# Retention and neighbourhood stages of a two-block fp32 model: a pair's last norm deferred, bias tables and residual rows requested earlier

## The chip, the core and the metric

The program runs on one core of one Trainium2 chip. The metric is the device time of one execution in microseconds (us); the kernel before takes 3239.62 us, the median of 3 runs (3238.14 to 3244.05). Everything is fp32 in and out. A projection is split into rounded high and low parts, and three matmuls (high by high, high by low, low by high) make one.

## The reference, cut

Two blocks on a sequence of 1024 tokens and 1024 channels. The first (dilated attention, then a state-space layer) is not touched. The second has two hybrid layers, each with a convolution branch, a retention branch (6 heads of 64) and a neighbourhood attention branch (6 heads), on 1024 tokens and 256 context tokens; in the second layer the context has only keys and values.

```python
def head_norm(o):
    mu = jnp.mean(o, axis=-1, keepdims=True)
    var = jnp.mean(jnp.square(o - mu), axis=-1, keepdims=True)
    return (o - mu) * lax.rsqrt(var + LN_EPS)

# retention: queries and keys rotated, both directions, chunks of 128
o = bidir_retention(qh, kh, vh, lg_f, lg_b, s_f, s_b)
y_ret = from_heads(head_norm(o)) * jax.nn.silu(g)

# neighbourhood: window of 8 x 16 on the 16 x 64 grid, plus all context tokens
s_loc = einsum(q, k_win) * scale + rpb[:, dr + 7, d_col + 15]
s_ctx = einsum(q, k_ctx) * scale
p = softmax(concatenate([s_loc, s_ctx]))
y_na = (einsum(p_loc, v_win) + einsum(p_ctx, v_ctx)) * silu(g)

y = concatenate([y_conv, y_ret, y_na]) @ w_out
x_new = layer_norm(DEEPNORM_ALPHA * x + gate * y, ln_g, ln_b)
```

## The kernel before

The program is written for a framework that lays the instructions of each engine out with a timeline of its own, so the order in the code is a wish: what an engine gets can stand some places earlier or later. TensorE (PE) does the matmuls and the transposes, VectorE (DVE) and ScalarE (ACT) read PSUM and write SBUF, GpSimd (POOL) helps, and all DMAs go out on the in-order queue of SyncE (SP).

Nearly all of TensorE's work is projections: `mm3` (the matmuls are line 168) issues 24 matmuls of 128x512 (or 128x256 for the context) into one PSUM tile `mm`, which has two buffers. After every eighth matmul it calls `tick()`, which runs a closure of the list `hot` and, at the speed that `pace()` set, closures of the list `bg`: so the small steps of attention are strewn between the projections. `drain()` runs what is left in `bg` at once.

`hybrid(l)` is called for l = 0 (with context) and l = 1 (without context queries). After half of the convolution it runs `ret_pair(p)` for three pairs of heads. `ret_pair` first projects the gates (and ticks the background of the pair before), then drains, then projects values, keys and queries. `raw` evicts a projection into `raw` (four buffers) and hangs the follow-up into `hot`. Each of a pair's query groups (two of 512 tokens, and for l = 0 one of 256 context tokens) has five steps f1 to f5, which become the background of the *next* pair's gates: f1 and f2 rotate and transpose (lines 1463, 1494), f3 makes the scores (line 1588) and f4 the outputs (1603, 1606). The end of f4 is a chain over four engines: copy `oe` (ACT, 1609), transposes `O` (PE, 1612), squares (ACT, 1617), row sums (DVE, 1619), two small POOL steps (1620, 1621), `cen` (DVE, 1623). f5 is the next step: PE transposes `cen` (1632), DVE multiplies by the gate (1635) and SP stores `yd` (1636). At the end of a gate projection `drain()` puts the last f4 and the last f5 right behind each other.

After pair 2, `na_project(0)` projects gates, values, keys (`nk`) and queries (`nqq`, line 1428) of the neighbourhood branch, and `na_core(p)` runs pairs 0 to 2: `vturn` and `cturn` transpose the values (PE 1677 and 1684; DVE copies `nV` 1678 and `nVc` 1686). `tables(rt)` brings a bias table for row type rt: one `mask` (one buffer) and six pieces of `tab` (tab0 and tab1, two buffers each, line 1700), and then DVE adds the mask (1701). Eight units of 128 queries follow: scores `S` (PE 1734), DVE 1710 and 1714 (which reads `tab`), ACT 1717 (exponential), transposes `T` (PE 1747, 1748), copies `nPT` (DVE 1751, ACT 1753), products `O` (PE 132, 135).

`out_ln` (from line 1916) ends the layer: for each tile of 128 tokens it fetches `x` (line 1949), projects two halves of 512 channels, multiplies each by `gate` out of PSUM (DVE 1955), adds the residual and keeps a row sum (1956), and normalises (1967 to 1972).

```python
self.bg.extend(late[g][k] for g, k in turns if g < len(late))
...
out = [tables(0), vturn(0), vturn(1), cturn, vturn(2), vturn(3)]
...
if i == 2:
    tables(1)()
```

## Time and profile before

| | before |
|---|---|
| median of 3 runs | 3239.62 us (3238.14 to 3244.05) |
| the profiled execution, its own time | 3247.39 us |
| its span, first to last instruction | 3245.4 us |
| TensorE busy | 3119.8 us, 96% of the span |
| VectorE, ScalarE, GpSimd busy | 59%, 37%, 18% |
| mean granted TensorE clock | 0.986 |
| second block, layer 0 and layer 1 | from about 1770 to 2560 us, and on to the end |

The span is read from its densest engine. TensorE is hardly ever idle, so what counts is the list of waits in front of its instructions, and for each of them what the other engines did at that moment. "[4.13 <-DVE cen L1623]" behind an instruction says that its engine sat idle for 4.13 us before it and that DVE's instruction of line 1623, which writes `cen`, ended that. An SP row's duration is the time in which the queue issued the transfer, not the time until it landed.

### The profile page before, as it was taken

To read this page: it belongs to the slowest core of one execution; us is meant where nothing else is said; L and a number is where in the kernel's file an instruction comes from. 1 tells how busy PE (TensorE), PEld (TensorE's weight loads), DVE (VectorE), ACT (ScalarE), POOL (GpSimd) and SP (SyncE) were. 2 spreads that over 40 slices of the span, in tenths; PEclk is the share of its full clock that TensorE was granted. 3 is DMA by queue.
4 is the path that set the end of the run, shared out by engine and by line. 5 is a ranking of instruction groups with operands and counts; after the bars stand their busy time and mean duration, and the time that the engine had idled before them with its cause. 6 is when DMAs were issued, how large, how long until landed. Compare 5 with 4: busy or idle time off the path is not lost. (4 is left out here: it accounts for less than half of the span.)

```text
span 3245.4 us, 48179 instructions
## 1 busy us (share of the span) xinstructions
PE 3119.8 (96%) x18340; PEld 2576.7 (79%) x18340; DVE 1925.1 (59%) x4147; ACT 1210.5 (37%) x2496; POOL 578.3 (18%) x769
## 2 busy tenths in 40 slices
PE   7999999999999999999999999999999999999998
PEld 6888787877778788787878888778887888778777
DVE  5565668777775748565644634454557854445555
ACT  4544444444444554322432122244352212134351
POOL 1244402121111201111003023200002212210001
PEclk9999999999999999999999999999999999999999
DMA  4222233332322225565342211142224321133232
GB/s 137 59 86 91 83 92 100 97 95 87 99 88 72 74 90 179 182 176 156 130 136 91 66 46 50 48 119 73 73 80 161 101 69 56 46 101 88 72 113 97
DMA packets 325210, 312.86 MB, mean 96 GB/s; under 512 B 27801, under 2 KB 277364, under 8 KB 324980
## 3 DMA queue, kind: packets, MB, share of 16 engines
q1 hardware_dynamic: 324980, 309.80, 31.4%
q8 instruction: 144, 2.36, 0.3%
q14 instruction: 86, 0.70, 0.1%
HBM read 249.64 MB, written 60.09 MB: 95 GB/s over the span
## 5 line engine op out<-in xcount | busy, mean ns | idle before, releaser
L168 PE MATMUL mm<-aTh,wh 128*128 128x512 f32 (+1 forms) x2704 | 1076.6, 398 | 26.6 <-DVE qk L353 9.8
L168 PE MATMUL mm<-aTl,wh 128*128 128x512 f32 (+1 forms) x2704 | 1075.0, 398 | 0.7 <-DVE aTl L221 0.3
L168 PE MATMUL mm<-aTh,wl 128*128 128x512 f32 (+1 forms) x2704 | 1070.1, 396 | 0.8 <-DVE wl L155 0.8
L168 PEld LDWEIGHTS mm<-aTh,wh 128*128 128x128 f32 x2704 | 513.4, 190 | 136.4 <-issue 8.2
L168 PEld LDWEIGHTS mm<-aTh,wl 128*128 128x128 f32 x2704 | 513.2, 190 | 102.6 <-issue 3.7
L168 PEld LDWEIGHTS mm<-aTl,wh 128*128 128x128 f32 x2704 | 513.8, 190 | 100.6 <-issue 5.4
L155 DVE TENSOR_TENSOR wl<-wr,wh 128x1024 fp32r<-128x1024 f32 x176 | 220.9, 1256 | 183.8 <-ACT wh L154 181.9
L154 ACT ACTIVATE wh<-wr 128x1024 fp32r<-128x1024 f32 x176 | 186.0, 1057 | 362.9 <-PE mm L168 297.7
L414 ACT ACTIVATE sb<-sb,st 128x128 f32<-128x128 f32 (+1 forms) x384 | 170.4, 445 | 278.3 <-DVE st L412 277.0
L168 PE MATMUL mm<-wo,aTh 128*128 128x512 f32 x768 | 242.4, 397 | 7.9 <-DVE ys L1955 4.6
L412 DVE CUSTOM_DVE_ANT_0 sb<-S,bt 128x128 f32<-128x128 f32 (+1 forms) x384 | 126.4, 343 | 116.9 <-PE T L425 92.3
L1153 DVE SCALAR_TENSOR_TENSOR ma<-mw,cact,ma 128x256 f32<-128x256 f32 x336 | 174.0, 530 | 15.6 <-DMA mw<-in_w_mod 10.0
L168 PEld LDWEIGHTS mm<-wo,aTh 128*128 128x128 f32 x768 | 144.5, 190 | 38.7 <-DVE ys L1955 5.0
L168 PE MATMUL mm<-wo,aTl 128*128 128x512 f32 x384 | 151.8, 395 | 0.9 <-DVE aTl L1900 0.9
L1717 ACT ACTIVATE nsb<-nsb,nmn 128x640 f32<-128x640 f32 (+1 forms) x108 | 85.6, 793 | 117.9 <-DVE nmn L1714 105.5
L1160 POOL TENSOR_TENSOR ms<-ma,ms 128x256 fp32r<-128x256 f32 x48 | 40.2, 837 | 413.9 <-ACT ms L1159 301.8
L357 POOL CAST qk<-kz 64x512 fp32r<-64x512 f32 x64 | 65.8, 1028 | 252.7 <-ACT kz L351 250.6
L425 PE MATMUL T<-ident,sb 128*128 128x128 f32 x560 | 99.3, 279 | 11.9 <-ACT PT L428 8.1
L168 PE MATMUL mm<-cTh,wl 128*128 128x256 f32 x352 | 101.9, 289 | 0.6 <-DVE wl L155 0.6
L168 PE MATMUL mm<-cTl,wh 128*128 128x256 f32 x352 | 102.0, 290 | 0.0
L168 PE MATMUL mm<-cTh,wh 128*128 128x256 f32 x352 | 101.4, 288 | 0.0
L1710 DVE CUSTOM_DVE_ANT_0 nsb<-S,zero 128x256 f32<-128x256 f32 x108 | 45.0, 421 | 84.2 <-PE T L1748 30.3
(443 smaller groups left out, 5221.1 us busy)
## 6 DMA issues: line engine op xcount, KB each, us to landing
wr<-in_attn_w_in SPq DMA_DIRECT2D x80, 512.0 KB
wr<-in_w_in SPq DMA_DIRECT2D x64, 512.0 KB
mw<-in_w_mod SPq DMA_DIRECT2D x48, 512.0 KB
tab<-in_c_rpb SPq DMA_DIRECT2D x72, 192.0 KB
Wb<-wgd SPq DMA_DIRECT2D x96, 128.0 KB
x<-x SPq DMA_DIRECT2D x24, 512.0 KB
x<-in_x SPq DMA_DIRECT2D x16, 512.0 KB
wr<-in_ssm_w_in SPq DMA_DIRECT2D x16, 512.0 KB
```

Of the source, the lines that this page charges most:

```text
L154: nc.scalar.activation(h, raw, AF.Copy)
L155: nc.vector.tensor_tensor(l, raw, h.bitcast(F32), op=ALU.subtract)
L168: nc.tensor.matmul(out, s_, m_, start=first and i == 0, stop=last and i == len(todo) - 1)
L357: nc.gpsimd.tensor_copy(at(t[o], g, hf), at(h_[r], g, hf))
L412: nc.vector.tensor_tensor_reduce(out=sb[:, :N], in0=sp[:, a * 256:a * 256 + N], in1=b, scale=1.0, scalar=3e38, op0=ALU.add, op1=ALU.min, a ...
L414: nc.scalar.activation(sb[:, :N], sb[:, :N], AF.Exp, bias=mc, scale=-1.0, accum_out=st[:, 1, g, a, n:n + 1])
L425: nc.tensor.transpose(t[:, c:c + 128], Ps[a][:, b * 128:b * 128 + 128], self.ident)
L1153: V.scalar_tensor_tensor(a, L[h][:, k], c, a, op0=ALU.mult, op1=ALU.add)
L1160: nc.gpsimd.tensor_tensor(l_, L["a", i], h.bitcast(F32), op=ALU.subtract)
L1710: V.tensor_tensor_reduce(out=sb[:, 0:256], in0=C, in1=zero.to_broadcast([128, 256]), scale=-0.125, scalar=3e38, op0=ALU.add, op1=ALU.min, ...
L1717: ACT.activation(sb[:, :n], sb[:, :n], AF.Exp, bias=mc, scale=-1.0, accum_out=den)
```

## The change

Three parts, all in the second block.

- **The last f5 of a pair waits.** `ret_pair` keeps the last step of the last query group in `tail`. The next pair puts it into the background again behind three empty closures, after its gates and its drain, at one closure for each tick: so it comes beside the next pair's values. Behind pair 2 it goes in front of `na_project(0)`, whose pace is 11 (8 without context) instead of 9 (6). The order `turns` of the steps changes slightly.
- **Tables requested ahead.** A new `fetch(p, rt)` issues the mask and the six pieces of a table; `tables(rt)` only adds the mask. The first fetch stands in front of `na_core(0)`, the second row type is fetched at unit 0 (its mask was fetched and added at unit 2, and is now added at unit 3), the next pair's first at unit 5. The mask still has one buffer and each `tab` two.
- **Residual.** `out_ln` requests the `x` rows of the next tile one tile ahead, and writes both halves' product with `gate` before it adds the residual to either.

```diff
+                    if tail:
+                        self.bg.extend([idle, idle, idle, tail.pop()])
+                        self.rate = 1.0
                     raw(values, True)
...
-                    turns = ((0, 0), (0, 1), (1, 0), (0, 2), (0, 3), (1, 1), (2, 0), (0, 4), (1, 2), (1, 3), (2, 1),
-                             (1, 4), (2, 2), (2, 3), (2, 4))
-                    self.bg.extend(late[g][k] for g, k in turns if g < len(late))
+                    turns = ((0, 0), (0, 1), (0, 2), (1, 0), (0, 3), (1, 1), (2, 0), (1, 2), (0, 4), (1, 3), (2, 1),
+                             (2, 2), (1, 4), (2, 3), (2, 4))
+                    turns = [t for t in turns if t[0] < len(late)]
+                    self.bg.extend(late[g][k] for g, k in turns[:-1])
+                    tail.append(late[-1][4])
 
                 for p in range(3):
                     ret_pair(p)
-                self.pace(9 if need_ctx else 6)
+                self.bg.extend([idle, idle, idle, tail.pop()])
+                self.pace(11 if need_ctx else 8)
                 na_project(0)
                 self.drain()
...
+                def fetch(p, rt):
+
+                    mask = wp.tile([128, 3, 384], F32, name=self.uid("mask"), tag="mask")
+                    nc.sync.dma_start(mask, A["c_namask"][:, rt * 3:rt * 3 + 3])
+                    ts = []
+                    for a in range(2):
+                        t = wp.tile([128, 3, 384], F32, tag=f"tab{a}", name=self.uid("tab"), bufs=2)
...
+                            nc.sync.dma_start(t[:, y], src)
+                        ts.append(t)
+                    TB[p, rt] = mask, ts
+                fetch(0, 0)
...
                     def tables(rt):
+                        mask, ts = TB.pop((p, rt))
+                        for a, t in enumerate(ts):
+                            V.scalar_tensor_tensor(t, t, 8.0, mask, op0=ALU.mult, op1=ALU.add)
+                            L["tab", rt, a] = t
...
-                    out = [tables(0), vturn(0), vturn(1), cturn, vturn(2), vturn(3)]
+                    out = [vturn(0), vturn(1), cturn, vturn(2), vturn(3), lambda: tables(0)]
...
-                            if i == 2:
-                                tables(1)()
+                            if i == 0:
+                                fetch(p, 1)
+                            if i == 3:
+                                tables(1)
+                            if i == 5 and p < 2:
+                                fetch(p + 1, 0)
...
+            if n < len(tiles):
+                xh = fetch()
             tt = slice(i * 128, i * 128 + 128)
             s = p.tile([128, 4], F32, tag="ls", name=self.uid("ls"))
             for nh in range(2):
                 c = slice(nh * 512, nh * 512 + 512)
                 ps = self.out_tile(i, nh, range(8), aT)
                 V.tensor_tensor(hs[:, c], ps, B["gate"][:, c], op=ALU.mult)
+            for nh in range(2):
+                c = slice(nh * 512, nh * 512 + 512)
                 V.scalar_tensor_tensor(hs[:, c], x[:, c], alpha, hs[:, c], op0=ALU.mult, op1=ALU.add,
                                        accum_out=s[:, nh:nh + 1])
```

How the built programs differ, at three places.

**TensorE, layer 1, from pair 1 to pair 2.** `O` are the transposes of f4, `T<-cen` those of f5, `T<-raw` the next pair's values, `mm` a projection's matmul. Before:

```order
L1606 MATMUL S_24968<-qw_4340_24925,St_24719 64x128
L1632 MATMUL T_24931<-ident,cen_24902 128x128 x4
L1606 MATMUL S_24968<-qw_4341_24928,St_24720 64x128
L1612 MATMUL O_24987<-ident,oe_24985 128x128 x4
L1632 MATMUL T_25002<-ident,cen_24998 128x128 x4
L1463 MATMUL T_25054<-ident,raw_25043 128x128 x4
L1463 MATMUL T_25090<-ident,raw_25079 128x128 x4
L168 MATMUL mm_25305<-aTh,wh_25117 128x512
```

Now, with the 24 matmuls of one projection (22 of them left out here) between `O` and `T<-cen`:

```order
L1611 MATMUL S_24968<-qw_4341_24928,St_24720 64x128
L1468 MATMUL T_25047<-ident,raw_25036 128x128 x4
L1617 MATMUL O_24987<-ident,oe_24985 128x128 x4
L168 MATMUL mm_25305<-aTh,wh_25117 128x512
...
L168 MATMUL mm_25305<-aTh,wl_25118 128x512
L1637 MATMUL T_25056<-ident,cen_24998 128x128 x4
L1468 MATMUL T_25090<-ident,raw_25079 128x128 x4
L1468 MATMUL T_25132<-ident,raw_25115 128x128 x2
```

Line 1612 is now 1617, 1632 is 1637, 1463 is 1468. Nothing stood between `O` and the transposes of `cen` before; a projection does now. The same holds for layer 0: 13 matmuls of 128x256 and 24 of 128x512 between pairs 0 and 1, and 15 of 128x256 with f3 and f4 work of another group between pairs 1 and 2.

**SP, layer 0, the first neighbourhood pair.** `yd<-sgl` is f5's store (1636, now 1641), `tab` and `mask` the tables. Before:

```order
L1636 DMA yd_16423<-sgl_19179 128x512
L148 DMA wr_19572<-in_w_in 128x8x128
L1381 DMA sgl_19995<-sgd_16424 128x512
L1691 DMA mask_19583<-in_c_namask 128x1152
L1700 DMA tab_19585<-in_c_rpb 128x1x384
L1636 DMA yd_16423<-sgl_19259 128x256
L1700 DMA tab_19585<-in_c_rpb 128x1x384 x2
L1700 DMA tab_19590<-in_c_rpb 128x1x384 x3
L1700 DMA tab_19751<-in_c_rpb 128x1x384 x3
L1700 DMA tab_19756<-in_c_rpb 128x1x384 x3
L148 DMA wr_19930<-in_w_in 128x8x128
L1691 DMA mask_19749<-in_c_namask 128x1152
```

Now:

```order
L148 DMA wr_19582<-in_w_in 128x8x128
L1641 DMA yd_16423<-sgl_19179 128x512
L1381 DMA sgl_20005<-sgd_16424 128x512
L1681 DMA mask_19566<-in_c_namask 128x1152
L1691 DMA tab_19568<-in_c_rpb 128x1x384
L1641 DMA yd_16423<-sgl_19259 128x256
L1691 DMA tab_19568<-in_c_rpb 128x1x384 x2
L1691 DMA tab_19572<-in_c_rpb 128x1x384 x3
L1691 DMA tab_19669<-in_c_rpb 128x1x384 x3
L1691 DMA tab_19673<-in_c_rpb 128x1x384 x3
L148 DMA wr_19930<-in_w_in 128x8x128
L1376 DMA sgd_16424<-sg_19625 128x512
```

The eleven other pieces still stand behind the store of the last f5 (now the deferred one), and the second mask behind one more store. In layer 1 the order is the same again, but for a gate store `sgd<-sg` that stood in the middle of the tables and now stands ahead of the first mask.

**VectorE, layer 0, the first tiles of `out_ln`.** Before:

```order
L1955 TENSOR_TENSOR ys_22426<-mm_22429,gate_22413 128x512
L1900 TENSOR_TENSOR cTl<-ys_22399,cTh 128x256
L1955 TENSOR_TENSOR ys_22426<-mm_22456,gate_22413 128x512
L1900 TENSOR_TENSOR cTl<-ys_22399,cTh 128x1536
L1900 TENSOR_TENSOR aTl<-ys_22392,aTh 128x256
L1956 SCALAR_TENSOR_TENSOR ys_22426,ls_22428<-ys_22426 128x512 x2
L1900 TENSOR_TENSOR aTl<-ys_22392,aTh 128x6x256
L1967 SCALAR_TENSOR_TENSOR ys_22426<-ys_22426,ls_22428,nsc_22415 128x1024
L1955 TENSOR_TENSOR ys_22483<-mm_22486,gate_22413 128x512
L1955 TENSOR_TENSOR ys_22483<-mm_22513,gate_22413 128x512
```

Now (1955 is 1986, 1956 is 1989, 1900 is 1924, 1967 is 2000):

```order
L1986 TENSOR_TENSOR ys_22413<-mm_22431,gate_22415 128x512
L1924 TENSOR_TENSOR cTl<-ys_22399,cTh 128x256
L1986 TENSOR_TENSOR ys_22413<-mm_22457,gate_22415 128x512
L1924 TENSOR_TENSOR cTl<-ys_22399,cTh 128x1536
L1924 TENSOR_TENSOR aTl<-ys_22392,aTh 128x256
L1989 SCALAR_TENSOR_TENSOR ys_22413,ls_22430<-ys_22413 128x512 x2
L1924 TENSOR_TENSOR aTl<-ys_22392,aTh 128x6x256
L2000 SCALAR_TENSOR_TENSOR ys_22413<-ys_22413,ls_22430,nsc_22417 128x1024
L1986 TENSOR_TENSOR ys_22428<-mm_22488,gate_22415 128x512
L1986 TENSOR_TENSOR ys_22428<-mm_22514,gate_22415 128x512
```

The rows are the same: the framework's timeline had already put both products in front of both additions. TensorE's and SP's order in `out_ln` doesn't move in either layer.

## Rows read from the trace of the kernel before

**Rows 1.** The chain that ended last, two pieces: start us, us, what

```profile
2789.35 6.21 PE mm L168 x21
2797.14 7.74 PE mm L168 x34
```

**Rows 2.** Waits of PE over the whole run: us in total, times, longest us

```profile
PE T L1632 <- DVE cen L1623: 9.6, 3, 4.1
...
PE mm L168 <- DVE ys L1955: 4.6, 1, 4.6
...
PE T L1747 <- DVE nPT L1751: 3.6, 1, 3.6
PE T L1748 <- DVE nV L1678: 3.2, 1, 3.2
...
PE mm L168 <- DVE nk L1428: 2.7, 1, 2.7
...
PE mm L168 <- DVE nqq L1428: 1.7, 1, 1.7
PE T L1747 <- DVE nV L1678: 1.7, 1, 1.7
PE T L1463 <- POOL rq L1494: 1.6, 1, 1.6
```

**Rows 3.** Timeline of PE, layer 0, pair 0 to pair 1

```profile
1956.34 0.69 PE L1632 MATMUL T<-ident,cen 128*128 128x128 f32 x2 [2.62 <-DVE cen L1623]
```

**Rows 4.** Timeline of PE, layer 0, pair 1 to pair 2

```profile
2034.69 0.44 PE L1612 MATMUL O<-ident,oe 128*128 128x128 f32 x2 [0.53 <-ACT oe L1609]
2037.96 0.69 PE L1632 MATMUL T<-ident,cen 128*128 128x128 f32 x2 [2.83 <-DVE cen L1623]
...
2040.19 0.80 PE L168 MATMUL mm<-aTh,wh 128*128 128x512 f32 x1
```

**Rows 5.** Timeline of PE, layer 1, pair 1 to pair 2

```profile
2781.55 0.66 PE L1612 MATMUL O<-ident,oe 128*128 128x128 f32 x4 [0.75 <-ACT oe L1609]
2786.33 1.11 PE L1632 MATMUL T<-ident,cen 128*128 128x128 f32 x4 [4.13 <-DVE cen L1623]
...
2789.00 0.79 PE L168 MATMUL mm<-aTh,wh 128*128 128x512 f32 x1
```

**Rows 6.** The stretch from 2780 us: us, busy of PE, PEld, DVE, ACT, POOL, clock, DMA

```profile
2780.00:2793.00 13.00, 8.12 (x33) 6.32 (x32) 5.61 (x9) 2.17 (x4) 1.83 (x2) 0.74 0.40 121
```

**Rows 7.** Timeline of PE, layer 1, pair 2's scores

```profile
2835.40 1.16 PE L1588 MATMUL S<-qT,kT 64*128 64x128 f32 x8 [1.16 <-DVE St L1552]
...
2839.00 0.80 PE L168 MATMUL mm<-aTh,wh 128*128 128x512 f32 x1 [1.76 <-ACT nv L1403]
```

**Rows 8.** Timeline of DVE, layer 0, first neighbourhood pair

```profile
2140.61 1.36 DVE L1701 SCALAR_TENSOR_TENSOR tab<-tab,mask 128x1152 f32<-128x1152 f32 x1 [2.26 <-DMA tab<-in_c_rpb]
...
2151.64 2.63 DVE L1701 SCALAR_TENSOR_TENSOR tab<-tab,mask 128x1152 f32<-128x1152 f32 x2 [6.75 <-DMA mask<-in_c_namask]
```

**Rows 9.** Timeline of SP's queue, layer 0, first neighbourhood pair

```profile
2130.84 0.32 SPq L1636 DMA_DIRECT2D yd<-sgl  x1
2131.20 8.11 SPq L1700 DMA_DIRECT2D tab<-in_c_rpb  x11
...
2141.99 2.63 SPq L1691 DMA_DIRECT2D mask<-in_c_namask  x1
```

**Rows 10.** Timeline of DVE, layer 1, first neighbourhood pair

```profile
2892.52 1.36 DVE L1701 SCALAR_TENSOR_TENSOR tab<-tab,mask 128x1152 f32<-128x1152 f32 x1 [2.52 <-DMA tab<-in_c_rpb]
...
2902.59 2.63 DVE L1701 SCALAR_TENSOR_TENSOR tab<-tab,mask 128x1152 f32<-128x1152 f32 x2 [4.74 <-DMA wr<-in_w_in]
```

**Rows 11.** Timeline of SP's queue, layer 1, first neighbourhood pair

```profile
2883.09 1.14 SPq L1376 DMA_DIRECT2D sgd<-sg  x1
...
2893.90 0.33 SPq L1691 DMA_DIRECT2D mask<-in_c_namask  x1
```

**Rows 12.** The chain that ended last, a transfer of table pieces

```profile
3043.14 5.45 DMA tab<-in_c_rpb
```

More of the change, by code (lines that the diff above doesn't have):

```diff
@@ L1445, in hybrid, with idle @@
                 size = (4, 4, 2)
+                tail = []
+                def idle():
+                    pass
                 def ret_pair(p):
@@ L1663, in hybrid @@
                 kind = (0, 1, 1, 2)
+                TB = {}
+                def fetch(p, rt):
[4 more added lines that the diff above has]
+                        t = wp.tile([128, 3, 384], F32, tag=f"tab{a}", name=self.uid("tab"), bufs=2)
+                        for y in range(3):
+                            dr = (0 if rt == 0 else 4) - 8 * rt + 7
+                            dc = (0, -8, -16)[y] + 15
+                            off = rpb.offset + (l * 6 + 2 * p + a) * 896 + (6 + dr) * 32 + dc - 239
+                            src = bass.AP(tensor=rpb.tensor, offset=off, ap=[[32, 8], [1, 16], [1, 384]])
+                            nc.sync.dma_start(t[:, y], src)
+                        ts.append(t)
+                    TB[p, rt] = mask, ts
+                fetch(0, 0)
                 def na_core(p):
@@ L1688, in tables @@
                     def tables(rt):
-                        def f():
-                            mask = wp.tile([128, 3, 384], F32, name=self.uid("mask"), tag="mask")
-                            nc.sync.dma_start(mask, A["c_namask"][:, rt * 3:rt * 3 + 3])
-                            for a in range(2):
-                                t = wp.tile([128, 3, 384], F32, tag=f"tab{a}", name=self.uid("tab"), bufs=2)
-                                for y in range(3):
-                                    dr = (0 if rt == 0 else 4) - 8 * rt + 7
-                                    dc = (0, -8, -16)[y] + 15
-                                    off = rpb.offset + (l * 6 + hd[a]) * 896 + (6 + dr) * 32 + dc - 239
-                                    src = bass.AP(tensor=rpb.tensor, offset=off, ap=[[32, 8], [1, 16], [1, 384]])
-                                    nc.sync.dma_start(t[:, y], src)
-                                V.scalar_tensor_tensor(t, t, 8.0, mask, op0=ALU.mult, op1=ALU.add)
-                                L["tab", rt, a] = t
-                        return f
+                        mask, ts = TB.pop((p, rt))
+                        for a, t in enumerate(ts):
+                            V.scalar_tensor_tensor(t, t, 8.0, mask, op0=ALU.mult, op1=ALU.add)
+                            L["tab", rt, a] = t
                     def soft(C, Lc, tab, den):
@@ L1930, in out_ln, with fetch @@
         pend = None
+        def fetch():
+            ctx, i = tiles[n]
+            xh = slab((2 - n if need_ctx else n + 2) % 3, [128, 2, 1024])
+            nc.sync.dma_start(xh[:, 0], (xc_src if ctx else x_src)[i * 128:(i + 1) * 128, :])
+            return xh
+        xh = fetch()
         for ctx, i in tiles:
@@ L1945, in out_ln @@
             aT = (self.cTh, self.cTl) if ctx else (self.aTh, self.aTl)
-            xh = slab((2 - n if need_ctx else n + 2) % 3, [128, 2, 1024])
             n += 1
             x, hs = xh[:, 0], xh[:, 1]
-            nc.sync.dma_start(x, src[i * 128:(i + 1) * 128, :])
+            if n < len(tiles):
+                xh = fetch()
             tt = slice(i * 128, i * 128 + 128)
```

## The prediction

> **What bounds the kernel now.** I read the shares of busy time first: TensorE is busy for 96% of the span, so only what stands in front of a TensorE instruction costs time. The chain of waits gives its pace: 34 matmuls of 128x512 in 7.74 us [rows 1], 0.228 us each. Context matmuls are half as wide; I count 0.12 us each, about half of that. Then I read TensorE's waits over the whole run [rows 2]. The biggest that the change can reach is the one of f5's transposes for `cen`: 9.6 us in 3 pieces. The timelines show them at the seams of the retention pairs: 2.62 us [rows 3], 2.83 us [rows 4] and 4.13 us [rows 5], the last two behind smaller waits of `O` for the copy `oe` (0.53 and 0.75 us).
>
> A wait has a second price. In the 13 us around the seam of rows 5 the mean granted clock is 0.74 [rows 6]; the clock has two levels, 2.4 and 1.2 GHz, and behind the idle piece it is at the lower one. There 21 matmuls take 6.21 us where 34 take 7.74 later on [rows 1]: 6.21 − 21 × 0.228 = 1.4 us lost. The 12 transposes in front of them take from 2786.33 to 2789.00, 2.67 us [rows 5]; half of it, 1.3, goes to the clock as well. A restart costs 2.7 us there. In layer 0 ten transposes take from 2037.96 to 2040.19, 2.23 us [rows 4], of which half, 1.1, is lost; behind them I count nothing.
>
> **Part 1, the deferred f5.** How long `cen` takes is the distance from `O` to `T<-cen`: 2037.96 − 2034.69 = 3.27 us for a context group [rows 4], 2786.33 − 2781.55 = 4.78 us for a full one [rows 5]. The order listings say what TensorE has to do meanwhile.
> - Layer 0, pair 0 to 1: 13 × 0.12 + 24 × 0.228 = 7.0 us of matmuls against 3.27 needed. The wait of 2.62 and the 1.1 of clock go. I keep 0.5 for a new short wait: the values of three groups now share their turn with f5, and `raw` and `T` have few buffers. Gain 2.62 + 1.1 − 0.5 = 3.2 (bounds 0 and 3.7).
> - Layer 0, pair 1 to 2: 15 × 0.12 = 1.8 us and part of another group's f3 and f4, worth some 2: 3.8 against 3.27 for `cen`, which is thin. Of 0.53 + 2.83 + 1.1 = 4.5 I take 3.1 (bounds 0 and 4.5): the wait for `oe` stays, and 0.9 for being late.
> - Layer 1, pair 1 to 2: 24 × 0.228 = 5.5 us against 4.78. Of 0.75 + 4.13 + 2.7 = 7.6 I take 6.6, leaving 1.0 for `oe` or `raw` (bounds 3 and 7.6). Layer 1, pair 0 to 1 has no such wait (the three of [rows 2] are the seams above) and gives nothing.
> - Pair 2 to the neighbourhood projections, layer 0: a transpose waits 1.6 us there for POOL's `rq` [rows 2]. The f5 steps go 3 to 24 matmuls later, so TensorE has the same work in another order; POOL isn't relieved. 0.7 (bounds 0 and 1.6).
> - Layer 1, pair 2: the second eight score matmuls wait 1.16 us for the state `St`, and the next projection 1.76 us for the copy `nv` [rows 7], with a restart of up to 2.7 between them. Both come from one DVE backlog: its `St` steps stood in front of two of the four `nv` copies. The pair's keys and queries now run 24 matmuls (5.5 us for the most part) later against the neighbourhood values, so that in DVE's order all four copies stand ahead of most `St` steps, and half of the second scores go later still. 1.16 + 1.76 and two thirds of the restart, 4.6 (bounds 0 and 5.6).
>
> The step moves a DMA as well: the store `yd` goes out behind f5. Behind it on SP stand, at the first two seams, loads of weights that have four buffers; I cost them at nothing, hidden by those buffers, and if that cover were gone each seam would lose the delay, at most the 5.5 us of a projection. At the third seam stand the tables.
>
> **Part 2, the tables.** Before, eleven of the twelve pieces of a layer's first tables leave behind f5's store: the store goes at 2130.84, the pieces from 2131.20 on, 8.11 us for issuing them [rows 9]. The order listing shows the same order after the change. So the request is written earlier, but the queue isn't free earlier: the store waits for f5, f5 is now put off, and by the place of its transposes goes out between 6 matmuls (1.4 us) and 17 (3.9 us) later.
> - Layer 0: `nqq` waits 1.7 us [rows 2] behind DVE's table addition, which itself sat idle 2.26 us for a piece [rows 8]. DVE's order now has `nqq` between the two additions, and this 1.7 goes. The 3.2 us of `T` for `nV` [rows 2] stay or grow: both additions of the second type stand in front of that copy, and wait for a mask that has one buffer; it left at 2141.99 [rows 9] and was awaited until 2151.64 [rows 8], 9.65 us. Later by 1.4 with the store: 1.7 − 1.4, rounded to 0 (bounds −3.9 and +4).
> - Layer 1: the gate store `sgd`, which left at 2883.09 [rows 11] between the table pieces, now stands ahead of all of them, so the pieces leave later. The scores that need the first table come 28 matmuls (6.4 us) later too. The two waits of `T`, 1.7 for `nV` and 3.6 for `nPT` [rows 2], hang on DVE's waits for a piece, 2.52, and for the mask, 4.74 [rows 10]. I take 2, the first of the two waits (bounds −6.3, if the pieces are that late and nothing covers it, and +6).
> - Later pairs: the same order on SP, but for single rows; 0 (bounds −2.5 and +2.5). The wait of `nk`, 2.7 us [rows 2], stays: its table piece is on the way for 5.45 us [rows 12], and its issue waits for a `tab` buffer as before.
>
> The Trainium skill (DMA: Bandwidth & Descriptors, Anatomy of one DMA) says that a semaphore wait is held by the issuing sequencer before dispatch, and the same page's Rules for kernel authors advise to issue a DMA early and to wait for it late, so that its fixed cost is overlapped. By the second sentence the tables would be free, and the sum would be that of the rival "ahead" below; by the first a request behind a waiting store isn't early, and the 0.36 us between store and pieces agrees. The page's fit (2.0 us and bytes by 436 GB/s, given for the gpsimd path) would make an estimate of 2.45 us for a piece of 192 KB; the 5.45 us of the row disagrees, and the row is used.
>
> **Part 3, the residual.** The order listings of `out_ln` are the same on TensorE, DVE and SP: 0. The wait of a projection for the `gate` product, 4.6 us [rows 2], stays. If the listing misled, 4.6 and a restart of 2.7 would go, 7.3 in all; nothing is added, so the lower bound is 0.
>
> **The sum.** 3.2 + 3.1 + 6.6 + 0.7 + 4.6 + 0 + 2 + 0 = 20.2 us less. Against the profiled execution's own 3247.39 this gives 3227.2. That execution is 7.8 us above the median of the runs, so against 3239.62 I forecast **3219.4 us**. A measurement of this kernel can tell about 0.2%, 6.5 us, from no change.
>
> **The rivals.**
> - *The waits only move.* f5's chain goes over ACT, DVE, POOL and DVE again, each in its own order; a projection's evictions and weight splits (1.22 us each on DVE) can come between, and `cen` is late again behind the thin cover at layer 0's second seam and in layer 1. For it: 0.5 us of slack at the one (3.8 − 3.27) and 0.7 at the other (5.5 − 4.78). Against: a late `cen` then costs what is missing, not the whole. With a third of 12.9 kept at the seams (4.3), 1.7 from the rest and no restart saved, 6.0: 3233.6, near the bound of what can be told. 18%.
> - *The tables become the bound, and it is slower.* The mechanism is SP's queue: all pieces stand behind the deferred store, in layer 1 behind the gate store too, and the one mask behind both additions. If the delay isn't covered, layer 0's first neighbourhood pair pays 3.9 us, layer 1's 6.3 us, and each of the four table waits becomes long enough for a restart, 4 × 2.7 = 10.8. What TensorE gains just ahead (0.7, 4.6, 2) is lost too, for a table's landing is set by the queue. 21.0 − 12.9 at the seams = 8.1 slower: 3247.7. It decides once the pieces land later than the scores that read them, 6.4 us in layer 1. Against it: only the three stall positions of before stand close to that. 10%.
> - *Ahead.* The requests really run ahead of the store on the chip, and masks too: the 1.7 and 3.2 of layer 0 with a restart (7.6) and the rest of layer 1's 1.7, 3.6 and 2.7 (6.0) go as well: 20.2 + 13.6 = 33.8, 3205.8. Against it stands the order listing. 8%.
>
> **How the numbers follow.** The forecast's own case, most seams relieved and the tables about even, has 64%: bounds of the seam terms taken half way give −11 to −27, 3213 to 3229. For 8 in 10 I go down to 3203, which takes in "ahead", and up to 3242, which takes in "the waits only move" with the tables a little worse; "slower" and a little on either side stay out. Faster by over 0.2%: the forecast, "ahead", and a part of the 18% that falls on that side, less a little of the forecast, 72%. Within 0.2%: the rest of "the waits only move", and forecasts halved by late tables, 17%. Slower: 11%.
>
> **What would show it.** In the profile after: TensorE's wait of `T` for `cen` falls from 9.6 us in 3 to under 1.5; after each seam the clock stays at its upper level, so the 13 us around layer 1's seam read over 0.9. The wait of `nqq` is gone, the one of the `gate` product is still some 4.6 us, and the second mask of layer 0 is still awaited for over 5 us. I am wrong if `T` still waits for `cen` over 4 us in all (the deferral covers nothing), if the waits of DVE for tables, 2.26 to 6.75 us now [rows 8, 10], are gone (then the requests do come early), or if the wait for the `gate` product is gone.

## The result

The changed kernel takes 3224.65 us (median of 6 runs, 3220.79 to 3230.23) against 3243.44 us for the kernel before in the same series (6 runs, 3238.14 to 3250.18). The ratio is 0.9944, with a 95% interval of 0.9928 to 0.9959: 18.8 us faster, where 20.2 were forecast. (The 3219.4 us of the forecast were counted from 3239.62, the median of the first three of these six runs.) The profiled execution of the changed kernel took 3227.41 us with a span of 3225.5 us, 20.0 us less than the profiled one of before; 3227.2 had been forecast for it.

TensorE's waits over the whole run, in the changed kernel (line 1637 is 1632 of before, 1617 is 1612, 1767 and 1768 are 1747 and 1748, 1986 is 1955); they answer to [rows 2]:

```profile
PE mm L168 <- ACT nv L1403: 7.3, 2, 5.7
PE T L1768 <- DVE nV L1709: 6.4, 1, 6.4
...
PE mm L168 <- DVE ys L1986: 3.5, 1, 3.5
...
PE T L1468 <- POOL rq L1499: 1.5, 1, 1.5
...
PE T L1637 <- DVE cen L1628: 0.5, 1, 0.5
```

The transposes of f5 waited 9.6 us for `cen`, and now wait 0.5. The wait of `nqq` and the one of the scores for `St` are gone from the list. Among the long ones stand two waits that were smaller before: `T` for `nV`, 3.2 us then and 6.4 now, and a projection for the copy `nv`, 5.7 at the longest. Both belong to the first neighbourhood pairs, in layer 0 and in layer 1. The 1.5 us for `rq` are not the 1.6 of before. That wait, in layer 0 between pair 2 and the neighbourhood projections, is gone, and a projection waits there for `nv` instead (the first row below). The 1.5 us are a new wait in layer 1's pair 2 (the second):

```profile
2085.16 0.50 PE L168 MATMUL mm<-aTh,wh 128*128 128x512 f32 x1 [1.66 <-ACT nv L1403]
...
2817.75 0.66 PE L1468 MATMUL T<-ident,rq 128*128 128x128 f32 x4 [1.49 <-POOL rq L1499]
```

At the seam of layer 1, the timeline of TensorE in the changed kernel, to be held against [rows 5]:

```profile
2772.24 0.66 PE L1617 MATMUL O<-ident,oe 128*128 128x128 f32 x4 [0.17 <-ACT oe L1614]
...
2778.34 0.60 PE L1637 MATMUL T<-ident,cen 128*128 128x128 f32 x4
...
2779.73 0.44 PE L1468 MATMUL T<-ident,raw 128*128 128x128 f32 x2 [0.35 <-DVE sgl L1640]
```

and `cen` itself, on VectorE:

```profile
2776.28 0.69 DVE L1628 TENSOR_TENSOR cen<-O,hv 128x512 f32<-128x512 f32 x1 [2.04 <-POOL hv L1626]
```

`cen` is no faster: it ends 4.73 us behind the start of `O` (2776.97 − 2772.24), where 2786.28 − 2781.55 = 4.73 was the distance in the trace of before. But TensorE now has 24 matmuls to do meanwhile, and they end at 2778.3, 1.3 us behind `cen`. Of the short wait expected for `raw` or `T`, 0.35 us came. The clock stayed up; the stretches around the seam of layer 1 and the first and second of layer 0, each from before `O` to behind `T<-cen` (columns as in [rows 6], where 0.74 was granted):

```profile
2771.00:2784.00 13.00, 12.48 (x68) 10.02 (x67) 6.02 (x11) 2.69 (x5) 1.83 (x2) 1.00 0.43 122
1945.00:1962.00 17.00, 16.92 (x104) 13.85 (x103) 6.42 (x11) 3.40 (x6) 1.79 (x6) 1.00 0.24 71
2022.00:2038.00 16.00, 14.76 (x101) 12.46 (x100) 6.72 (x13) 3.07 (x6) 5.08 (x10) 1.00 0.27 81
```

At layer 0's second seam, from pair 1 to pair 2, the order is not the one that the prediction reckons with:

```profile
2025.12 0.60 PE L1617 MATMUL O<-ident,oe 128*128 128x128 f32 x4
...
2029.93 0.66 PE L1637 MATMUL T<-ident,cen 128*128 128x128 f32 x4 [0.55 <-DVE cen L1628]
2030.42 0.38 PE L1617 MATMUL O<-ident,oe 128*128 128x128 f32 x2
...
2037.51 0.38 PE L1637 MATMUL T<-ident,cen 128*128 128x128 f32 x2
```

The deferred f5 is that of the context group, with two transposes. Between its `O` (2030.42) and its `T<-cen` (2037.51) stand 24 matmuls of 128x512, and it doesn't wait. The 15 matmuls of 128x256 with f4 work stand one group earlier, between the `O` (2025.12) and the `T<-cen` (2029.93) of the second full group. All of the 0.5 us that is left of the wait for `cen` is there.

The tables are another matter. VectorE and SP in the first neighbourhood pair of layer 0, changed kernel, against [rows 8, 9] (`sgd<-sg` is the store of a gate):

```profile
2134.18 1.36 DVE L1722 SCALAR_TENSOR_TENSOR tab<-tab,mask 128x1152 f32<-128x1152 f32 x1 [2.27 <-DMA tab<-in_c_rpb]
...
2147.20 2.63 DVE L1722 SCALAR_TENSOR_TENSOR tab<-tab,mask 128x1152 f32<-128x1152 f32 x2 [9.20 <-DMA mask<-in_c_namask]
```

```profile
2119.95 0.70 SPq L1691 DMA_DIRECT2D tab<-in_c_rpb  x1
2123.98 0.32 SPq L1641 DMA_DIRECT2D yd<-sgl  x1
2124.35 7.62 SPq L1691 DMA_DIRECT2D tab<-in_c_rpb  x11
2134.11 4.28 SPq L1376 DMA_DIRECT2D sgd<-sg  x1
2138.48 0.38 SPq L1681 DMA_DIRECT2D mask<-in_c_namask  x1
```

The queue stood 3.3 us (2120.65 to 2123.98) before the deferred store, with eleven pieces behind it. In the trace of before it stood there for 9.9 us, from the end of the first piece's row to the store at 2130.84 [rows 9]:

```profile
2120.28 0.70 SPq L1700 DMA_DIRECT2D tab<-in_c_rpb  x1
```

Against TensorE's work little moved: counted in projection matmuls from the start of the program, the pieces leave 3 matmuls later than before. The second mask left at 2138.48 and was awaited until 2147.20, 8.7 us. A gate store stands in front of it now, and the row of that store is 4.28 us long; so the mask leaves 2.9 us behind the additions that free its buffer (2134.18 + 1.36 = 2135.54). Before, it left right behind them, though its own row took 2.63 us [rows 9]; what makes these rows long no run shows. `nqq` no longer waits behind a table addition, and VectorE stood idle for the mask from 2138.00 on, 9.20 us instead of 6.75.

In layer 1, against [rows 10, 11], where the first addition of before, which isn't among those rows, comes first here:

```profile
2887.77 1.36 DVE L1701 SCALAR_TENSOR_TENSOR tab<-tab,mask 128x1152 f32<-128x1152 f32 x1 [4.40 <-DMA tab<-in_c_rpb]
```

and in the changed kernel

```profile
2870.38 1.36 DVE L1722 SCALAR_TENSOR_TENSOR tab<-tab,mask 128x1152 f32<-128x1152 f32 x1 [7.14 <-DMA tab<-in_c_rpb]
...
2873.62 1.36 DVE L1722 SCALAR_TENSOR_TENSOR tab<-tab,mask 128x1152 f32<-128x1152 f32 x1
...
2884.62 2.63 DVE L1722 SCALAR_TENSOR_TENSOR tab<-tab,mask 128x1152 f32<-128x1152 f32 x2 [5.89 <-issue]
2887.16 0.42 DVE L1404 COPY nv<-mm 128x256 f32<-128x256 f32 x1
```

```profile
2860.26 0.32 SPq L1376 DMA_DIRECT2D sgd<-sg  x1
...
2862.68 0.41 SPq L1641 DMA_DIRECT2D yd<-sgl  x1
2863.14 8.78 SPq L1691 DMA_DIRECT2D tab<-in_c_rpb  x11
...
2875.01 0.33 SPq L1681 DMA_DIRECT2D mask<-in_c_namask  x1
```

and SP's wait in front of that gate store, over 2840 to 2910 us:

```profile
SPq L1376 <- ACT sg L1375: 3.5, 1, 3.5
```

The gate store went ahead of the mask and of all twelve pieces, and held the queue for 3.5 us, until ScalarE had written `sg`. Counted in projection matmuls, the pieces leave 16 later than before. TensorE doesn't wait for them directly. But the second mask is requested when the second addition has ended (2873.62 + 1.36 = 2874.98), so late pieces make a late mask: it left at 2875.01, 15 matmuls later than before. What the row calls "issue" is taken here for this mask again; the additions began 9.6 us behind its request. The copies of `nv`, one of which stands right behind the additions, are what TensorE waits 5.7 us for. No run takes the gate store alone out of the way, so its share of this isn't known. Behind both long waits the clock falls: in the 15 us from 2140 (layer 0) and from 2880 (layer 1) 0.70 and 0.77 were granted.

**Where the time went, stretch by stretch.** To compare two executions I worked out a loss for each stretch between two given matmuls: every TensorE instruction's distance to the next one's start, less the median distance for its width in the trace of before (0.227 us for 512 columns, 0.120 for 256), summed up. Ends of stretches are the same matmul, counted, in both traces.

| stretch | us, before | loss before | loss after | change | forecast |
|---|---|---|---|---|---|
| first block and layer 0's convolution | 17 to 1945 | 50.2 | 49.6 | −0.6 | 0 |
| layer 0, pair 0 to 1 | 1945 to 2027 | 2.1 | −1.0 | −3.1 | −3.2 |
| layer 0, pair 1 to 2 | 2027 to 2062 | 5.3 | 1.9 | −3.4 | −3.1 |
| layer 0, to the neighbourhood projections | 2062 to 2137 | −0.2 | 0.0 | +0.2 | −0.7 |
| layer 0, first neighbourhood pair | 2137 to 2223 | 11.7 | 11.2 | −0.6 | 0 |
| later pairs, `out_ln` of layer 0 | 2223 to 2489 | 13.2 | 12.2 | −0.9 | 0 |
| layer 1, pair 1 to 2 | 2712 to 2801 | 5.9 | −1.9 | −7.8 | −6.6 |
| layer 1, pair 2 and projections | 2801 to 2892 | 5.3 | 0.5 | −4.9 | −4.6 |
| layer 1, first neighbourhood pair | 2892 to 2962 | 9.8 | 12.7 | +2.9 | −2 |
| layer 1, later pairs | 2962 to 3070 | 6.6 | 5.1 | −1.5 | 0 |

(2489 to 2712 and the end change by under 0.1.) The sum is −19.7 us. In the repeat of the changed kernel (the last run below) the two first neighbourhood pairs lost 9.7 and 12.0 instead of 11.2 and 12.7, so a change of 1.5 us in such a stretch can be the execution's.

### The profile page after: what moved, and what is told of

It is laid out like the page before. It is cut to its first block, busy times and chain, and to the rows that moved or that the text cites. A ratio compares the mean times of both kernels' runs of the same rounds, so it can differ in the third digit from the quotient of the medians.

```text
span 3225.5 us, 48176 instructions
## 1 busy us (share of the span) xinstructions
PE 3114.9 (97%) x18340; PEld 2573.5 (80%) x18340; DVE 1928.4 (60%) x4147; ACT 1207.5 (37%) x2494; POOL 585.6 (18%) x769
```

## The experiments

The theory on record holds that the seams carry the gain, by the distance that the deferral puts between `O` and `cen`'s transposes; that requesting tables ahead brings nothing, because the requests stand behind a waiting store; and that the residual's part changes nothing. The rivals were a share for the tables, a share for the residual, and a gain that doesn't depend on the distance. All runs were timed in five rounds, against the kernel before on the same chip.

**Each part alone.** The first three kernels are the kernel before with one part of the change, as the diff above shows it.

Part 1, the deferred f5. Expected:

> The kernel before with part 1 alone (the deferred f5 and its new order of steps). Theory S (the seams carry it): 17 to 22 us faster than before (ratio 0.993 to 0.995), TensorE's wait of T for cen under 1.5 us in all. Rival T (the requested-ahead tables carry a share): under 12 us faster. Rival Q (the deferred store costs at the tables, and asking ahead wins it back): like T, with longer waits at the tables of both first neighbourhood pairs than the changed kernel has.

Measured: 3229.18 us against 3247.06, ratio 0.9937 (0.9919 to 0.9956), 17.9 us. TensorE's wait for `cen`, and what stays:

```profile
PE mm L168 <- ACT nv L1403: 7.9, 2, 6.3
...
PE T L1759 <- DVE nV L1689: 5.3, 1, 5.3
...
PE T L1637 <- DVE cen L1628: 0.5, 1, 0.5
```

Part 1 alone is as fast as the whole change. It also brings the long waits at the tables by itself: they come from the deferral, not from the requests ahead. That speaks against a share for the tables (rival T) and against rival Q, in which asking ahead wins something back.

Part 2, the tables. Expected:

> The kernel before with part 2 alone (masks and tables requested ahead). Theory S: the store of f5 still stands in front of eleven pieces, so within 4 us of before, on either side; the three waits for cen stay at 9 to 10 us. Rival T: 6 to 14 us faster, and VectorE's idle time for tables, 54.7 us before, falls under 35.

Measured: ratio 0.9996 (0.9986 to 1.0007), no change. TensorE's waits and what VectorE waited for before a table addition (us, times):

```profile
PE T L1632 <- DVE cen L1623: 9.6, 3, 4.1
```

```profile
  DMA tab<-in_c_rpb: 53.6, 18
```

54.7 us of waiting for pieces of tables in 17 waits before, 53.6 in 18 here, 57.7 in 19 in the changed kernel: a request that is written earlier, behind a store that still waits, isn't an earlier request. In the built queue nothing came ahead: of SP's 1176 rows only a store `yd` and a load of weights, late in layer 1, changed places against the kernel before. TensorE's order did change, from layer 1's neighbourhood branch on. So this run shows that part 2 as written brings nothing; what tables that really leave earlier would bring it doesn't show.

Part 3, the residual. Expected:

> The kernel before with part 3 alone (next tile's x one ahead, both products before both additions). Theory S: no change, within 2 us, since the order on the engines is the same; TensorE's wait for the gate product stays at 3.5 to 4.8 us. Rival R (the residual's part does something that the order doesn't show): 4 to 8 us faster and that wait gone.

Measured: ratio 1.0006 (0.9993 to 1.0019), no change. The wait for the `gate` product in the first tiles of `out_ln`:

```profile
PE mm L168 <- DVE ys L1962: 3.1, 1, 3.1
```

It was 4.6 before and 3.1 to 4.0 in the other executions that keep this order: this much it moves from one execution to the next. In the traces of this kernel and of the kernel before, the rows of TensorE, ScalarE and SP stand in the same order from the first to the last, so part 3 left the built order as it was, and the 1.0006 is what two measurements of one order differ by.

**The distance.** The changed kernel without the three empty closures in `ret_pair` (those in front of `na_project(0)` stay):

```diff
-                        self.bg.extend([idle, idle, idle, tail.pop()])
+                        self.bg.extend([tail.pop()])
                         self.rate = 1.0
```

> The changed kernel, but the deferred f5 stands at the head of the background, without the three empty closures (one tick instead of four behind the start of the next values). Theory S: the order on TensorE is then that of before at all three seams, so the three waits for cen are back, 8 to 10 us with their restarts, and the time is within 5 us of before. Rival D (what counts is that another pair's gates come in between, not the distance): still over 12 us faster.

Measured: ratio 0.9995 (0.9983 to 1.0007). The whole gain is gone, and the waits at the seams are those of before to a tenth:

```profile
PE T L1637 <- DVE cen L1628: 9.6, 3, 4.1
```

The waits of `nqq` (1.9 us), of the scores for `St` (1.2) and of a projection for `nv` (2.0) are back too, so the gain in layer 1's pair 2 also hangs on these closures. The traces say why: all rows of TensorE (18340), VectorE, ScalarE and SP stand in the same order as in the run with part 2 alone. Without the closures part 1 isn't in the built order at all. So the 0.9996 there and the 0.9995 here are one order measured twice, and this run is no case of rival D, in which only gates come in between: here nothing does. With one or two closures (built, not run) the order is that of none, and with five that of three. At the seam f5 moves behind a whole projection of 24 matmuls or not at all; a distance in between wasn't to be had.

**The tables.** What sets the two long waits that are left? First the mask's one buffer: the second row type's mask gets a tile of its own for pairs 0 and 1.

```diff
+                ms = ExitStack()
+                mp = ms.enter_context(tc.tile_pool(name=self.uid("nm"), bufs=1, reuse_waits="tile"))
...
-                    mask = wp.tile([128, 3, 384], F32, name=self.uid("mask"), tag="mask")
+                    own = mp if rt and p < 2 else wp
+                    mask = own.tile([128, 3, 384], F32, name=self.uid("mask"), tag="mask")
...
+                ms.close()
```

> The changed kernel with a tile of its own for the second row type's mask (pairs 0 and 1 of each layer), so that this mask is requested among the first pair's tables instead of behind both table additions. Theory M (the one mask buffer sets the two long waits that are left in the first neighbourhood pairs): VectorE's waits for the mask (9.2 us in layer 0, some 5.9 in layer 1) fall under 3, TensorE's waits of 6.4 us (T for nV) and 5.7 us (mm for nv) fall under 2 each, and the kernel is 7 to 12 us faster than the changed one, 0.990 to 0.992 of before. Rival B (the transfers share the engines of the DMA and land when their bytes are through): the waits move to the tables that now share with the mask, under 4 us faster, 0.993 to 0.995 of before.

Measured: ratio 0.9944 (0.9926 to 0.9961), the changed kernel's own. No wait is put down to the mask any more (one of 2.3 us in layer 1 has no name); the pieces are waited for, and for longer (VectorE before a table addition, us, times):

```profile
  DMA tab<-in_c_rpb: 68.0, 21
```

and TensorE's waits in the two first pairs, 6.4 and 5.7 in the changed kernel, are now:

```profile
PE T L1770 <- DVE nV L1712: 3.8, 1, 3.8
PE T L1771 <- DVE nV L1712: 3.7, 1, 3.7
```

By stretches layer 0's first pair lost 9.4 instead of 11.2 us, layer 1's 17.1 instead of 12.7. Theory M, with its 7 to 12 us, falls: the buffer was what the wait was put down to, and without it the wait moves to the pieces beside the mask.

Then the store: behind pair 2 it is issued behind the first fetch.

```diff
+                            def store():
+                                nc.sync.dma_start(yd[256 + p * 128:384 + p * 128, g * 512:g * 512 + n * 128],
+                                                    sg[:, :n * 128])
+                            if p == 2 and g == (2 if need_ctx else 1):
+                                held.append(store)
+                            else:
+                                store()
...
                 fetch(0, 0)
+                held.pop()()
```

> The changed kernel with the deferred f5's store behind pair 2 issued behind the first six table pieces instead of ahead of eleven. Theory H (the waiting store at the head of SP's queue holds up the tables): layer 0's pieces leave some 4 us sooner and TensorE's wait of 6.4 us there shrinks by 2 to 4; layer 1, where the store left 0.1 us behind the first piece, does not change; 1 to 4 us faster than the changed kernel. Rival M (the mask's buffer sets it): both waits within 1 us of the changed kernel's.

Measured: ratio 0.9929 (0.9911 to 0.9946), against 0.9944 for the changed kernel; the intervals overlap, so the time alone doesn't decide. The queue and the waits of layer 0's first pair do:

```profile
2124.51 4.97 SPq L1697 DMA_DIRECT2D tab<-in_c_rpb  x6
2129.59 0.52 SPq L1643 DMA_DIRECT2D yd<-sgl  x1
...
2137.53 0.34 SPq L1687 DMA_DIRECT2D mask<-in_c_namask  x1
2137.97 0.38 SPq L1376 DMA_DIRECT2D sgd<-sg  x1
```

```profile
2136.14 1.36 DVE L1729 SCALAR_TENSOR_TENSOR tab<-tab,mask 128x1152 f32<-128x1152 f32 x1 [0.39 <-DMA tab<-in_c_rpb]
...
2146.29 2.63 DVE L1729 SCALAR_TENSOR_TENSOR tab<-tab,mask 128x1152 f32<-128x1152 f32 x2 [5.86 <-DMA mask<-in_c_namask]
```

The first six pieces leave in one go, VectorE's wait for the second table falls from 2.27 to 0.39 us and that for the mask from 9.20 to 5.86. The stretch lost 7.9 us instead of 11.2: 3.2 less, within what theory H expected for layer 0. In layer 1, where H expected nothing, 10.4 instead of 12.7. Against the repeat of the changed kernel, with 9.7 and 12.0, it is 1.8 and 1.6. Two things changed in layer 0's queue, though. The gate store, which stood in front of the second mask, stands behind it here. The mask leaves 0.03 us behind the additions (2136.14 + 1.36 = 2137.50) instead of 2.9, and is on its way as long as before (8.8 us until it is added, 8.7 in the changed kernel). So most of the 3.34 us by which VectorE's wait for the mask shrinks goes with the gate store's place, not with the deferred store at the head; this run doesn't part the two.

**The residual, forced.** On VectorE the first addition waits for `x` in front of the next tile's products, whatever the order in the code. Here the additions are tied behind the products of the second tile:

```diff
-                V.tensor_tensor(hs[:, c], ps, B["gate"][:, c], op=ALU.mult)
-            for nh in range(2):
...
+                product = V.tensor_tensor(hs[:, c], ps, B["gate"][:, c], op=ALU.mult)
+
+            def add(x=x, hs=hs, s=s):
...
+            adds.append(add)
+            if n > 1:
+                with self.tc.issue_after(product.ins):
+                    while adds:
+                        adds.pop(0)()
```

> The changed kernel with the residual of the first output tile forced behind the second tile's two products on VectorE (an explicit order, which the framework can't rearrange). Theory P (the first addition's wait for x blocks the products behind it, and TensorE waits for their PSUM): the wait of a projection for the gate product, 3.5 us, and its restart go; 3 to 6 us faster than the changed kernel. Rival X (VectorE's splits before the products, or x itself for the next step, set it): within 1.5 us of the changed kernel.

Measured: ratio 0.9926 (0.9908 to 0.9945). TensorE's wait there, and VectorE's rows:

```profile
PE mm L168 <- DVE ys L1987: 1.1, 1, 1.1
```

```profile
2447.42 1.29 DVE L1987 TENSOR_TENSOR ys<-mm,gate 128x512 f32<-128x512 f32 x2
2448.62 0.68 DVE L1992 SCALAR_TENSOR_TENSOR ys<-ys 128x512 f32<-128x512 f32 x1
```

The products come right behind the splits, and the addition finds its `x`. The stretch around it lost 3.8 us instead of 8.7 (8.4 in the repeat): 4.9 less, as theory P expects. By the times alone (0.9926 against 0.9944) the intervals overlap. This is what part 3 says and, in the program built from it, doesn't do.

**All three, and two controls.**

> The changed kernel with the three edits together: the second mask's own tile, the store behind the first six pieces, and the residual forced behind the products. Theory M with H and P: 10 to 18 us faster than the changed kernel, 0.988 to 0.991 of before. If only one of them holds: 3 to 8 us faster, 0.992 to 0.994.

Measured: 3217.96 us, ratio 0.9910 (0.9891 to 0.9929): the fastest here but for one that leaves work out. Against the changed kernel that is 0.0034 of 3244 us by the ratios, 11 us, the lower end of what was expected. Layer 0's first pair lost 6.1 us, `out_ln` of layer 0 3.9, layer 1's first pair 9.2, and 2.6 came back in layer 1's later pairs (7.7 instead of 5.1).

Without the second mask's tile:

> The changed kernel with the store behind the first six pieces and the residual forced behind the products, and one mask buffer as in the changed kernel. Theory B (the tables of the first neighbourhood pairs are bound by the bytes that the transfers bring, and a second mask buffer only moves waits): as fast as the kernel with all three edits, 0.990 to 0.992 of before. Theory M (the mask's buffer counts once the store is out of the way): 2 to 5 us slower than that one, 0.992 to 0.9935.

Measured: 3223.93 us, ratio 0.9931 (0.9917 to 0.9944), 5.3 us below the changed kernel run beside it. The intervals of this and of all three overlap; by stretches, the second block lost 39.4 us here and 39.0 with all three, so by the profiled executions the mask's tile moves waits and wins nothing, as theory B says, and by the medians it wins some, as theory M says. This stays open.

With the second mask's transfers left out (the first type's mask is added in their place):

> The kernel with all three edits, without the second row type's mask transfers: the first type's mask is added in its place, so the bias mask of half the rows is another one. Theory B: 576 KB less among the first pair's tables at the 180 to 190 GB/s that the profile shows there are 3 us; VectorE's waits for the second type's tables shrink by 1.5 to 3 us in each layer, and the kernel is 2 to 6 us faster than the one with all three edits. Rival I (it is the issue of the pieces on SP's queue, 0.6 us each, that sets it): waits within 1 us of that kernel's, the time within 1.5 us.

Measured: 3216.97 us, ratio 0.9908 (0.9893 to 0.9922), no different from all three in time. VectorE's waits for the second type's two tables in layer 0, with all three edits and then without those transfers:

```profile
2137.92 1.36 DVE L1732 SCALAR_TENSOR_TENSOR tab<-tab,mask 128x1152 f32<-128x1152 f32 x1 [1.25 <-DMA tab<-in_c_rpb]
2141.70 1.36 DVE L1732 SCALAR_TENSOR_TENSOR tab<-tab,mask 128x1152 f32<-128x1152 f32 x1 [2.43 <-DMA tab<-in_c_rpb]
```

```profile
2141.32 1.36 DVE L1735 SCALAR_TENSOR_TENSOR tab<-tab,mask 128x1152 f32<-128x1152 f32 x1 [1.51 <-DMA tab<-in_c_rpb]
2145.24 1.36 DVE L1735 SCALAR_TENSOR_TENSOR tab<-tab,mask 128x1152 f32<-128x1152 f32 x1 [0.76 <-issue]
```

3.68 us become 2.27, 1.4 less; in layer 1 the two waits are 2.02 + 2.26 = 4.28 with all three edits and 0.54 + 2.25 = 2.79 here, 1.5 less. That is at the lower edge of what theory B asked for and more than rival I allowed; the time does what rival I says. The bytes beside the pieces count, but not enough to see it in the time; how much of a piece's way is its own issue on the queue and how much is sharing isn't settled.

The changed kernel once more:

> The changed kernel once more, on the same chip as these runs: 0.993 to 0.996 of before, by every theory; it is there so that the others can be compared with it.

Measured: 3229.2 us, ratio 0.9944 (0.9930 to 0.9957), the first result again.

## Why the prediction was right

**The seams: right in size, right in mechanism at two of the three.** 3.2, 3.1 and 6.6 us were forecast, 3.1, 3.4 and 7.8 measured. Part 1 alone gives the whole gain, and without its closures the built order and the time are those of a kernel without part 1, so this is shown. The working that mattered was the comparison of 4.78 us of chain with 5.5 us of matmuls between `O` and `T<-cen`: chain 4.73, cover 6.1 from `O` to `T<-cen`. At layer 0's second seam the 3.1 us came out by luck. The section on the change names 15 context matmuls and f3 and f4 work there, and the prediction set them, 3.8 us, against the 3.27 of the deferred context group. In the built program that group has 24 matmuls of 128x512, and the 15 stand before the `T<-cen` of the full group ahead of it, whose chain is the longer one (2025.12 to 2029.93, 4.81 us with 0.55 of waiting). So 0.5 us of slack were 0.55 us of wait. With the 0.69 us that the first matmul behind the next `O` waited for `raw` (at 2031.92), 1.2 us came where 1.4 had been kept for other reasons. Layer 1 was sized 1.2 too small: of the whole microsecond kept for new waits only 0.35 and 0.17 us came; the other 0.7 wasn't traced to a row.

**Layer 1's pair 2: right.** 4.6 forecast (1.16 + 1.76 and two thirds of 2.7 make 4.7), 4.9 measured. The wait for `St` is gone from the list, and the wait for `nv` at that place too; the `nv` wait of 5.7 us in the list is another one, in the first neighbourhood pair. The new wait for `rq`, 1.49 us, was not foreseen.

**To the neighbourhood projections, layer 0: small miss.** 0.7 forecast, +0.2 measured. The wait for POOL's `rq` did go, all of its 1.6 us, but another took its place, 1.66 us of a projection for `nv`. The text had a gain from reordering there and no price for what the reordering would put in its way.

**The tables: right that they don't come ahead, wrong in layer 1's sign.** Layer 0 was put at 0 and came to −0.6. The delay of the store that was set there, 6 to 17 matmuls, was 3; the gate store in front of the second mask, which the section on the change names ("one more store"), wasn't in the sum. For layer 1 a gain of 2 was forecast and a loss of 2.9 measured. The step that failed is the one that took "the first of the two waits" off there: the first wait, for `nV`, did go from the list, but the pieces left 16 matmuls later behind the gate store and the second mask 15 later, and TensorE paid in front of that mask, whose addition on VectorE holds the copies `nv` behind it, 5.7 us. The bound of −6.3 to +6 held it. The later pairs of layer 1 gave 1.5 that nobody claimed.

**The residual: right.** Listings equal, 0 forecast, ratio 1.0006 for one and the same order. The forced version shows that the price put on that wait, 7.3 us at most with a restart, was of the right order: 4.9.

**The sum.** 20.2 forecast, 19.7 by stretches and 18.8 by the medians. That it came this close is in part luck: layer 1's tables were wrong by 4.9 us, and 1.2 us more at layer 1's seam and 3.6 us in stretches put at 0 made most of it up.

**The rivals.** "The waits only move" happened at the tables and with `rq` and `nv`, not at the seams. "The tables become the bound" named the right queue, stores and mask, and they did become the longest waits of the second block's attention. But the deferred store hardly delays the pieces (3 matmuls in layer 0; in layer 1 it left 0.1 us behind the first piece), and one long wait came in each layer, not four restarts, so it took back about 3 of 23 us, all in layer 1. "Ahead" didn't happen. Of what the text said would show it, the wait for `cen` (0.5, under 1.5), the clock (1.00, over 0.9), the wait of `nqq` (gone) and the mask (9.20, over 5) came out so; the wait for the `gate` product was 3.5 rather than 4.6, which is within what it varies by. The Trainium skill's advice to issue a DMA early (DMA: Bandwidth & Descriptors, Rules for kernel authors) would have given the tables' gain; the same page's sentence that the wait is held by the issuing sequencer (Anatomy of one DMA) is what the traces agree with: 3.3 us of queue in front of the deferred store in layer 0, and 3.5 us in front of the gate store in layer 1. No run here has the tables' requests ahead of both.

## What to carry to other kernels

When two steps of a chain over several engines meet on TensorE, put work of its own between them and compare two lengths read from the trace: the chain from its first to its last TensorE step, and the matmuls in between; here 4.7 against 5.5 us made 7.8 us of difference, clock included. A request for data is as early as the first waiting instruction in front of it in its queue, so read the queue's order before counting a prefetch, and look for every store in front of it: a gate store that changed its place counted here beside the deferred one. And check in the built order that an edit of the code moves what it is meant to move: part 3 moved nothing here, part 2 no table request, and part 1 without its three closures nothing either. Check too which group an instruction belongs to before setting a cover against a chain.

## What was not expected of the hardware

The part of the program that no kernel here touches, up to 1798 us, lost between 48.0 and 56.6 us in the 13 profiled executions shown here, with the same instructions in the same order. That is nearly half of the change, in one execution; only stretches, or medians of many runs, compare. The transfers have their share in it: the wait for the `gate` product behind `x` was between 3.1 and 4.6 us in executions with one order.

The wait that the profile names isn't always what sets the time: the row says that VectorE waited 9.20 us for the mask, but a mask that comes early left it waiting for the pieces beside it, 68.0 us in all instead of 57.7. Nor does it name what stood in front of the request: 2.9 of these 9.20 us passed before the mask was asked for, beside a gate store whose row took 4.28 us.
